# A two-layer attention trunk: x inside the first weight chunks, norms on VectorE by column halves, paired score products, attention steps in slots

## The chip, the cores and the metric

The kernel runs on one core of a Trainium2 chip. The metric is the device time of one execution in microseconds (us), as the median of runs; three runs of the kernel before gave 465.69, 466.3 and 468.05. Inside the core five engines work beside each other and wait for one another by semaphores: TensorE (PE, matmuls and transposes), VectorE (DVE), ScalarE (ACT), GpSimd (POOL) and SyncE (SP, which only issues DMAs here).

## The reference

A batch of one, 256 tokens of width 1024, and two layers in float32. The first layer runs retention (4 heads) and latent attention (8 heads whose scores have a 128-wide and a rotary 64-wide part) from one input projection; the second runs 16 heads of 64 columns, all of them causal over one block of 256 keys, so that no gathered block weighs anything. Both end in an output projection and a layer norm:

```python
def retention_mla_layer(x, pos, w_in, q_norm_g, w_uq, kv_norm_g, w_ukv, w_out):
    h = x @ w_in
    rq, rk, rv, rg, mq, mkv, mkr, mg = _split(h, EVEN_SPLITS)
    ...
    return jnp.concatenate([ret_out, mla_out], axis=-1) @ w_out

def moba_layer(x, pos, w_in, w_out):
    q, k, v, g = _split(x @ w_in, ODD_SPLITS)
    ...
    return (_merge(o) * jax.nn.silu(g)) @ w_out

for i in range(DEPTH):     # 2
    y = retention_mla_layer(...) if i % 2 == 0 else moba_layer(...)
    x = layer_norm(DN_ALPHA * x + y, ln_g[i], ln_b[i])
```

## The kernel before

**Arithmetic.** A float32 product is made of three passes: every operand is split into a high part (ACT copies it to a rounded type, L156) and a low part (DVE subtracts, L157), and `mm3` (L149 to L153) multiplies high by high (L151), low by high (L152 or L153, by which operand is which) and high by low. Weights are split in the same way as they arrive.

**Weights.** They are packed in the order of use into chunks of 512 KB (288 KB for the first eight). `load` (L169) fetches the next one on SP's queue into one of 4 raw buffers and splits it into one of 6 weight buffers, or into named spare ones.

**Start.** x comes transposed (`xt`) in four pieces of 256 KB on ACT's queue; eight chunks of 576 columns (queries' and keys' latents, tile names pm) are multiplied with it, 12 matmuls each. Constants, positions, norm gains and the decay table follow on ACT's queue, after the eight x splits in program order.

**Attention.** The small steps (scores, softmax, transposed probabilities, values) of retention, latent attention and the second layer are generators in one list `todo`; after each weight chunk of a projection `tick()` advances the first of them by one step, and `drain()` runs it empty. A scheduler of the framework then orders the instructions of each engine. The scores of a head (`causal_scores`, tile sc) are 3 passes for the first 128 queries against 128 keys and 3 for the second against 256; in latent attention each is followed by 3 passes of the rotary part, which has 64 contraction rows (kpe, qpe; two heads lie in the two halves of the 128 rows). In the second layer all score products have 64 rows (ck, cq).

**Output projections.** `out_proj` keeps the last TAIL = 4 chunks, does them for token tile 0 (128 tokens) first, then calls `between(0)`, which has tile 0's layer norm, and does them for tile 1 by pieces of columns. `layer_norm` divides its work by SPREAD: value 2 (tile 0 in either layer) squares on ACT and lets ACT and POOL do the second affine step, 1 (tile 1 of the first layer) squares on ACT alone, 0 (tile 1 of the second) is on DVE except for one power on POOL. In the first layer the normalised tile is transposed (pt, L708) and split into xT for the second layer, whose first five chunks (HOLD) are multiplied with tile 0 before tile 1 is needed. In the last call, tile 1's columns are done in pieces of 512, 256 and 256, each tile is normalised and stored in two halves on SP's and ACT's queues.

Of the kernel before, what the change touches and what calls it, by code (L numbers as in the profile page):

```python
# [32 lines left out]
TAIL = 4  # L33
HOLD = 5
WARM = 9
SPREAD = (2, 1, 2, 0)
# [9 lines left out]
def _plan():  # L46
    """The weight stream: per chunk its name, matrix, k tiles and columns."""
# [7 lines left out]
    block("m", "in0", _r(O_MQ, 256) + _r(O_MKR, 32) + _r(O_MKV, 256) + _r(O_MKR + 32, 32))  # L55
# [47 lines left out]
def _consts():  # L103
    """Constants of the shapes: identity, causal mask, decay tables, rotary frequencies."""
# [21 lines left out]
    return np.ascontiguousarray(np.concatenate(parts, 1))  # L126


CONSTS = _consts()
NCST = CONSTS.shape[1]  # L130
# [4 lines left out]
def trunk(ctx, tc, x, xt, pos, gq, gkv, lng, lnb, w, cst, dec, out):  # L135
# [13 lines left out]
    def mm3(o, a, b, ca, cb, start=False, stop=False):  # L149
        """o += a.T @ b by three passes of the split operands a, b (hi, lo)."""  # L150
        nc.tensor.matmul(o, ca(a[0]), cb(b[0]), start=start, stop=False, skip_group_check=True)  # L151
        nc.tensor.matmul(o, ca(a[1]), cb(b[0]), start=False, stop=False, skip_group_check=True)  # L152
        nc.tensor.matmul(o, ca(a[0]), cb(b[1]), start=False, stop=stop, skip_group_check=True)  # L153

    def split_to(hi, lo, src):
        nc.scalar.activation(hi, src, AF.Copy)  # L156
        nc.vector.tensor_tensor(lo, src, hi.bitcast(F32), op=OP.subtract)  # L157

# [8 lines left out]
    state = {"u": 0, "off": 0}  # L167

    def load(name, tags=None):  # L169
        tag, _, ks, cols = PLAN[state["u"]]  # L170
        assert tag == name, (tag, name)
        n = len(ks) * len(cols)
        raw = wp.tile([P, n], F32, name="raw", tag="raw", bufs=4)
        nc.sync.dma_start(raw, bass.AP(tensor=w.tensor, offset=w.offset + state["off"], ap=[[n, P], [1, n]]))
        state["u"] += 1
        state["off"] += n * P
        return ks, [t.rearrange("p (k c) -> p k c", c=len(cols)) for t in wsplit(raw, n, tags)]
# [8 lines left out]
    # work that waits for its turn between the chunks of the projections  # L186
    todo = []

    def tick(n=1):
        for _ in range(n):  # L190
            while todo:
                try:
                    next(todo[0])
                    break
                except StopIteration:
                    todo.pop(0)

    def drain():
        while todo:
            tick()  # L200
# [20 lines left out]
    pos_i = wk.tile([P, S], I32, name="pos_i", tag="neg", bufs=4)  # L221
    posn_i = cp.tile([P, NT], I32, name="posn_i")
    gqn = cp.tile([P, 2], F32, name="gqn")
    gkvn = cp.tile([P, 2], F32, name="gkvn")
# [8 lines left out]
    mask = cc("mask")  # L233

    # latent compression of queries and keys/values, shared rotary key
    pm = [[(pp, at)[j](f"pm{t}{j}") for j in range(2)] for t in range(NT)]
    xn = [cp.tile([P, DM], F32, name=f"xn{t}") for t in range(NT)]
    xr = [z.rearrange("p (k s) -> p k s", s=S) for z in xn]
    for k in range(0, KD, 2):
        nc.scalar.dma_start(xr[k // 4][:, k % 4:k % 4 + 2, :], xt[:, k:k + 2, :])  # L240
    for k in range(KD):
        split_to(xT_hi[:, k, :], xT_lo[:, k, :], xr[k // 4][:, k % 4, :])
        _, wv = load("m")
        for t in range(NT):
            for j in range(2):
                mm3(pm[t][j][:, :288], x_rows(k), wv, lambda z: z[:, t * P:(t + 1) * P],
                    lambda z: z[:, 0, j * 288:(j + 1) * 288], start=k == 0, stop=k == KD - 1)
    nc.scalar.dma_start(cs, cst)
    nc.scalar.dma_start(pos_i, bass.AP(tensor=pos.tensor, offset=pos.offset, ap=[[0, P], [1, S]]))
    for t in range(NT):  # L250
        nc.scalar.dma_start(posn_i[:, t:t + 1],
                            bass.AP(tensor=pos.tensor, offset=pos.offset + t * P, ap=[[1, P], [1, 1]]))
    nc.scalar.dma_start(gqn, gq)
    nc.scalar.dma_start(gkvn, gkv)
    nc.scalar.dma_start(decay, dec)

    def angles(dst_cos, dst_sin, ang, shape):
        """cos and sin of ang, brought to [-pi, pi] first."""
# [35 lines left out]
    def rope(src, t, nt, nh, dst, tag=None):  # L294
        """Half-split rotation of nh heads of 64 columns of nt token tiles from t on."""
# [13 lines left out]
    def transposed(srcs, n, hi, lo):  # L309
        """hi, lo (P, n, S) = the split transposes of the token tiles srcs[t] (P, n * P)."""  # L310
# [8 lines left out]
    lat = []  # L319

    def latents():
# [19 lines left out]
        yield  # L341
# [14 lines left out]
        yield  # L356
        pk = at("pk")
        for t in range(NT):
# [3 lines left out]
            nc.tensor.transpose(pk[:, t * P:(t + 1) * P], kd.rearrange("p a d -> p (a d)"), ident)  # L362
        lat.append(split(pk[:, :S], [P, S], "kpe"))
        yield
# [13 lines left out]
    def blockT_proj(name, o):  # L378
        """o (P, 2 * S) = the transpose of rows @ a block of 256 columns."""
# [9 lines left out]
    def gate(src, shape, name, bufs):  # L389
        """(tanh(g / 2) + 1) * g, twice silu(g)."""  # L390
# [5 lines left out]
    def rstd_of(stats, eps, half):  # L396
        """(var + eps) ** -0.5, halved where the gate is doubled, and -mean * that."""
# [11 lines left out]
    def retention(h, mid=None):  # L409
        """Projections of one retention head; its other steps go to todo as soon as they can."""  # L410
# [23 lines left out]
        def scores():  # L434
# [9 lines left out]
            yield  # L444

        def values():
            sT, v = got["sT"], got["v"]
# [12 lines left out]
            yield  # L460

        def merge():
            for t in range(NT):
                nc.vector.tensor_tensor(got["o"][t], got["o"][t], got["g"][t], op=OP.mult)
            hi = wk.tile([P, 4, S], F32R, name=f"rT{h}_h", tag="rT_h", bufs=2)
# [4 lines left out]
            yield  # L470

        todo.append(scores())
# [9 lines left out]
        todo.append(values())  # L482
# [3 lines left out]
        todo.append(merge())  # L486
# [26 lines left out]
    def causal_scores(o, prods):  # L513
        """o (P, 384) = scores of both query tiles; prods: (split queries, split keys, partitions)."""
        for t, a, n in ((0, 0, P), (1, P, S)):
            for i, (q, k, rs) in enumerate(prods):
                mm3(o[:, a:a + n], q, k, lambda y: y[rs, t * P:(t + 1) * P], lambda y: y[rs, :n],
                    start=t == 0 and i == 0, stop=i == len(prods) - 1)
# [8 lines left out]
    def av(o, pT, v, cols, start):  # L527
        """o (columns, S) = the transpose of probabilities @ values (of columns cols)."""
# [3 lines left out]
    def rotary_queries():  # L532
        """The rotary part of the queries of all latent-attention heads, transposed."""
# [14 lines left out]
        def later():  # L548
            transposed(qr, MH // 2, hi, lo)
            yield  # L550
        todo.append(later())
        tick()

    def mla(p):
        """Projections of a pair of latent-attention heads; the attention goes to todo."""
# [31 lines left out]
        def attend():  # L587
            sc = [at("sc") for a in range(2)]
# [261 lines left out]
```

## Time and profile before

| | |
|---|---|
| three runs | 465.69, 466.3 (median), 468.05 us |
| span of the profiled execution | 464.4 us; the page gives no other time of it |
| PE busy | 450.3 us, 97% |
| DVE, ACT, POOL busy | 73%, 51%, 3% |
| matmuls in the records | 2975 |
| HBM read | 74.01 MB |

The span runs from the first to the last instruction of the program; the time of a run also has what lies around it. A busy engine is one with an instruction in it: matmuls overlap, each lasts longer in the record than the distance to the next one, and so their pace is read from the distance of their starts.

### The profile page before, as it was taken

The numbers are of one execution on the slowest core, as the hardware profiler recorded it, in microseconds if no ns is written. First come the engines' busy times: TensorE is split into PE (matmuls) and PEld (weight loads), VectorE is DVE, ScalarE is ACT, GpSimd is POOL, SyncE is SP. The second block draws the span as 40 slices with busy tenths as digits, with TensorE's granted clock in tenths as the row PEclk, the third lists the DMA queues.
The fourth block names the chain that finished last, engine by engine and source line by source line (L and its number), as shares of the span: only waits on it lengthen the run. The fifth ranks groups of instructions, "written<-read, shape, count | busy, mean of one in ns | idle before, by whom it ended". The sixth has DMA issues, their size and how long they took to land.

```text
span 464.4 us, 7703 instructions
## 1 busy us (share of the span) xinstructions
PE 450.3 (97%) x2975; PEld 403.0 (87%) x2975; DVE 339.7 (73%) x658; ACT 236.0 (51%) x393; POOL 15.5 (3%) x22
## 2 busy tenths in 40 slices
PE   7999999999999999999999999999999999999993
PEld 4898899888999888889998888878999999999882
DVE  4889679785876866556596767655979798797836
ACT  5486464554644534345454646432646474644602
POOL 0010000000000000000000000020000000000003
PEclk9999999999989999999999999999999999999998
DMA  7987534544462556454445556824564435464002
GB/s 232 317 277 239 194 131 159 175 144 135 137 182 91 182 177 232 158 185 159 139 138 178 197 166 193 307 87 137 171 234 134 137 103 149 119 182 137 1 0 90
DMA packets 22787, 75.54 MB, mean 163 GB/s; under 512 B 3040, under 2 KB 3296, under 8 KB 22752
## 3 DMA queue, kind: packets, MB, share of 16 engines
q1 hardware_dynamic: 20016, 69.48, 46.6%
q10 hardware_dynamic: 2736, 5.59, 3.6%
q8 instruction: 23, 0.38, 0.3%
q14 instruction: 12, 0.10, 0.1%
HBM read 74.01 MB, written 1.05 MB: 162 GB/s over the span
## 4 chain that ended last, share of the span: by engine, by line
PE 94%; DMA 2%; DVE 2%; issue 0%; ACT 0%; DVEq 0%
PE pg L152 5%; PE pg L151 5%; PE pg L153 5%; PE pj L152 5%; PE pj L153 5%; PE pj L151 5%; PE acc L153 4%; PE acc L152 4%; PE acc L151 4%; PE pv L151 3%; PE pv L152 3%; PE pv L153 3%; PE pa L152 2%; PE pa L153 2%; PE pa L151 2%; PE sc L151 2%
## 5 line engine op out<-in xcount | busy, mean ns | idle before, releaser
L157 DVE TENSOR_TENSOR w_l<-raw,w_h 128x1024 fp32r<-128x1024 f32 (+2 forms) x134 | 157.6, 1180 | 64.0 <-ACT w_h L156 60.3
L156 ACT ACTIVATE w_h<-raw 128x1024 fp32r<-128x1024 f32 (+2 forms) x134 | 136.9, 1023 | 117.4 <-issue 38.0
L152 PE MATMUL pj<-w_h,xT_lo 128*128 128x256 f32 x192 | 54.3, 283 | 0.9 <-DVE xT_lo L157 0.9
L153 PE MATMUL pj<-w_l,xT_hi 128*128 128x256 f32 x192 | 54.3, 284 | 0.0
L151 PE MATMUL pj<-w_h,xT_hi 128*128 128x256 f32 x192 | 53.9, 284 | 0.0
L152 PEld LDWEIGHTS pj<-w_h,xT_lo 128*128 128x128 f32 x192 | 36.1, 188 | 1.1 <-DVE xT_lo L157 1.1
L153 PEld LDWEIGHTS pj<-w_l,xT_hi 128*128 128x128 f32 x192 | 36.1, 188 | 0.1
L151 PEld LDWEIGHTS pj<-w_h,xT_hi 128*128 128x128 f32 x192 | 35.8, 188 | 0.1
L151 PE MATMUL pv<-w_h,xT_hi 128*128 128x512 f32 x64 | 25.5, 399 | 0.0
L152 PE MATMUL pg<-w_h,xT_lo 128*128 128x512 f32 x64 | 25.4, 398 | 0.0
L152 PE MATMUL pv<-w_h,xT_lo 128*128 128x512 f32 x64 | 25.4, 397 | 0.0
L153 PE MATMUL pv<-w_l,xT_hi 128*128 128x512 f32 x64 | 25.4, 397 | 0.0
L153 PE MATMUL pg<-w_l,xT_hi 128*128 128x512 f32 x64 | 25.3, 399 | 0.0
L151 PE MATMUL pg<-w_h,xT_hi 128*128 128x512 f32 x64 | 25.3, 395 | 0.0
L500 DVE CUSTOM_DVE_ANT_0 neg<-sc,cs 128x128 f32<-128x128 f32 (+1 forms) x48 | 14.9, 355 | 9.4 <-PE sc L153 9.2
L503 ACT ACTIVATE prob<-neg,csm_m 128x128 f32<-128x128 f32 (+1 forms) x32 | 14.1, 443 | 11.0 <-DVE csm_m L500 11.0
L152 PE MATMUL pq<-xT_hi,w_l 128*128 128x256 f32 x64 | 18.5, 288 | 0.8 <-DVE w_l L157 0.8
L151 PE MATMUL pq<-xT_hi,w_h 128*128 128x256 f32 x64 | 18.8, 294 | 0.1
L152 PE MATMUL pkk<-xT_hi,w_l 128*128 128x256 f32 x64 | 18.6, 290 | 0.0
L151 PE MATMUL pkk<-xT_hi,w_h 128*128 128x256 f32 x64 | 18.6, 290 | 0.0
L153 PE MATMUL pkk<-xT_lo,w_h 128*128 128x256 f32 x64 | 18.5, 289 | 0.0
L152 PE MATMUL pg<-xT_hi,w_l 128*128 128x256 f32 x64 | 18.4, 287 | 0.0
(295 smaller groups left out, 1212.1 us busy)
## 6 DMA issues: line engine op xcount, KB each, us to landing
raw<-w SPq DMA_DIRECT2D x125, 512.0 KB, 3.6
raw<-w SPq DMA_DIRECT2D x8, 288.0 KB, 5.0
xn<-xt ACTq DMA_DIRECT2D x4, 256.0 KB, 7.1
raw<-w SPq DMA_DIRECT2D x4, 256.0 KB, 2.8
xn<-x ACTq DMA_DIRECT2D x2, 512.0 KB, 3.8
decay<-dec ACTq DMA_DIRECT2D x1, 512.0 KB, 5.0
decay_ln<-lng ACTq DMA_DIRECT2D x1, 512.0 KB, 4.2
rv_h_ln<-lnb ACTq DMA_DIRECT2D x1, 512.0 KB, 4.7
```

The source lines that it names most:

```text
L151: nc.tensor.matmul(o, ca(a[0]), cb(b[0]), start=start, stop=False, skip_group_check=True)
L152: nc.tensor.matmul(o, ca(a[1]), cb(b[0]), start=False, stop=False, skip_group_check=True)
L153: nc.tensor.matmul(o, ca(a[0]), cb(b[1]), start=False, stop=stop, skip_group_check=True)
L156: nc.scalar.activation(hi, src, AF.Copy)
L157: nc.vector.tensor_tensor(lo, src, hi.bitcast(F32), op=OP.subtract)
L500: nc.vector.tensor_tensor_reduce(out=neg[:, :b - a], in0=sc[j][:, a:b], in1=mask[:, S - b + a:], scale=-scale, scalar=3e38, op0=OP.add, op ...
L503: nc.scalar.activation(prob[:, j, a:b], neg[:, :b - a], AF.Exp, bias=nm[:, i, j:j + 1], scale=-1.0, accum_out=sm[:, i, j:j + 1])
```

## The change

- **x and constants.** x's eight 256-column pieces stand in front of the weights of the first chunks: 9 fetches, of 256 + 288, 288 and 7 times 832 columns, all issued at once on SP's queue into 4 raw buffers and 6 others. Positions and norm gains become columns of the constant table. Its DMA and the decay table's are issued on ACT's queue behind x's split number 2 and number 4.
- **Slots.** Every entry of `todo` has a tick at which it may go on; a generator yields how many ticks to wait (LAT1 to CAV) and 0 where an input is missing. Its step is issued after the last matmul so far.
- **Scores.** `causal_scores` has the 128-row products alone. `paired_scores` does the 64-row products of two heads, alternating between them.
- **Between the layers.** TAIL is 5. Tile 0's last chunks are multiplied by column halves too; the second layer's first five chunks are loaded before the norm of tile 0, and the last two chunks of tile 1's second half are issued after tile 0's transposes. `layer_norm` runs on DVE, each column half followed by its transposes; only tile 0 of the last norm squares on ACT.
- **End.** Tile 1's norm, affine steps and stores go by 512, 256 and 256 columns, and its first sum is issued after the affine step of tile 0 recorded in `state["normed"]`, which the call with t = 0 removes.

```diff
-TAIL = 4
+TAIL = 5
+LAT1, LAT2, QR, SCO, VAL, MRG, MSC, MPT, MAV, CROT, CSC, CPT, CAV = 3, 4, 2, 1, 1, 1, 1, 1, 1, 1, 1, 1, 1
-SPREAD = (2, 1, 2, 0)
...
+    def add(task, wait=1):
+        todo.append([state["tick"] + wait, task])
+    def tick():
+        state["tick"] += 1
+        for entry in list(todo):
+            if entry[0] > state["tick"]:
+                continue
+            try:
+                with tc.issue_after(state["mm"].ins):
+                    wait = next(entry[1])
+            except StopIteration:
+                todo.remove(entry)
+                continue
+            entry[0] = state["tick"] + (wait or 1)
+            if wait:
+                return
...
+    homes = [None] * 4 + [n + e for n in ("rqk", "mqk", "rv") for e in ("_h", "_l")]
+    first = [fetch("m", 0 if i == 1 else S, homes[i]) for i in range(KD + 1)]
+    for i, (raw, n, ks, cols) in enumerate(first):
+        k = ks[0]
+        if i != 1:
+            at_act = split_to(xT_hi[:, k, :], xT_lo[:, k, :], raw[:, :S])
+            for at_k, dst, src in ((2, cs, cst), (4, decay, dec)):
+                if k == at_k:
+                    with tc.issue_after(at_act.ins):
+                        nc.scalar.dma_start(dst, src)
...
+    def paired_scores(o, q, k, start):
+        for t, c, n in ((0, 0, P), (1, P, S)):
+            for i, (x, y) in enumerate(((0, 0), (1, 0), (0, 1))):
+                for a in range(2):
+                    rs = slice(a * MR, (a + 1) * MR)
+                    nc.tensor.matmul(o[a][:, c:c + n], q[x][rs, t * P:(t + 1) * P], k[y][rs, :n],
+                                     start=start and t == 0 and i == 0, stop=i == 2, skip_group_check=True)
...
         held = [load(name, spare[i] if i < len(spare) else None)[1] for i in range(last)]
-        for n in range(last):
-            part(n0 + n, held[n], 0)
+        ahead = [(n, load(n)) for n in nxt]
+        for cols in pieces[0]:
+            for n in range(last):
+                part(n0 + n, held[n], 0, cols)
         between(0, acc[0])
...
+            if "normed" in state:
+                with tc.issue_after(state.pop("normed").ins):
+                    return total(j, sl, **kw)
...
+        for j, sl in enumerate(parts):
+            if j > 1:
+                nc.vector.scalar_tensor_tensor(y[:, sl], y[:, sl], mv[:, 0:1], g[:, sl], op0=OP.subtract, op1=OP.mult)
+            state["normed"] = nc.vector.scalar_tensor_tensor(y[:, sl], y[:, sl], r[:, 0:1], b[:, sl],
+                                                             op0=OP.mult, op1=OP.add)
+            after(j, sl)
```

PE in the first layer, the scores of one pair of latent-attention heads: mqk is the 128-row part, 128x128 and 128x256 are the shapes of the outputs, kpe and qpe are the rotary 64-row part, `_h` and `_l` the high and low parts, and the number behind sc tells the head. Before:

```order
L153 MATMUL sc_2687<-mqk_l_2607,mqk_h_2606 128x128
L151 MATMUL sc_2687<-kpe_h_465,qpe_h_760 128x128
L152 MATMUL sc_2687<-kpe_h_465,qpe_l_761 128x128
L153 MATMUL sc_2687<-kpe_l_466,qpe_h_760 128x128
L151 MATMUL sc_2687<-mqk_h_2606 128x256
L152 MATMUL sc_2687<-mqk_h_2606,mqk_l_2607 128x256
L153 MATMUL sc_2687<-mqk_l_2607,mqk_h_2606 128x256
L151 MATMUL sc_2687<-kpe_h_465,qpe_h_760 128x256
```

Now, at the same place:

```order
L157 MATMUL sc_2681<-mqk_h_2599 128x256
L158 MATMUL sc_2681<-mqk_h_2599,mqk_l_2600 128x256
L159 MATMUL sc_2681<-mqk_l_2600,mqk_h_2599 128x256
L549 MATMUL sc_2680<-kpe_h_600,qpe_h_753 128x128
L549 MATMUL sc_2681<-kpe_h_600,qpe_h_753 128x128
L549 MATMUL sc_2680<-kpe_h_600,qpe_l_754 128x128
L549 MATMUL sc_2681<-kpe_h_600,qpe_l_754 128x128
```

The twelve 64-row products of a pair stood in four groups of three between 128-row products, and stand now in one group behind them, with the two heads in turn.

PE in the second layer, the first score products of two pairs of heads (ck and cq are keys and queries of 64 rows). Before:

```order
L151 MATMUL sc_3531<-ck_h_3420,cq_h_3412 128x128
L152 MATMUL sc_3531<-ck_h_3420,cq_l_3413 128x128
L151 MATMUL sc_3532<-ck_h_3420,cq_h_3412 128x128
L152 MATMUL sc_3532<-ck_h_3420,cq_l_3413 128x128
L151 MATMUL sc_3567<-ck_h_3420,cq_h_3412 128x128
```

Now:

```order
L549 MATMUL sc_3518<-ck_h_3407,cq_h_3399 128x128
L549 MATMUL sc_3519<-ck_h_3407,cq_h_3399 128x128
L549 MATMUL sc_3518<-ck_h_3407,cq_l_3400 128x128
L549 MATMUL sc_3519<-ck_h_3407,cq_l_3400 128x128
L549 MATMUL sc_3554<-ck_h_3407,cq_h_3399 128x128
```

The first pass of the second head moved ahead of the first head's second pass; what surrounds them is the same.

DVE at the end of the program: xn0 and xn1 are the two token tiles, acc the sums of the output projection, lmv and lr mean and scale of a norm, and lng, lnb its affine rows. Before:

```order
L658 SCALAR_TENSOR_TENSOR xn1_98<-xn1_98,acc_4915 128x512 [waits PE_49]
L654 TENSOR_SCALAR lr_5077<-lsm_5079 128x1 [waits Activation_49]
L666 SCALAR_TENSOR_TENSOR xn0_97<-xn0_97,lmv_5078,lng_ln1_3249 128x512 [waits DVE_49]
L666 SCALAR_TENSOR_TENSOR xn0_97<-xn0_97,lmv_5078,lng_ln1_3249 128x512
L660 BN_STATS lst_5135<-xn1_98 128x6 [waits DVE_49]
L658 SCALAR_TENSOR_TENSOR xn1_98<-xn1_98,acc_4916 128x512 [waits PE_49]
L660 BN_STATS lst_5135<-xn1_98 128x6 [waits DVE_49]
L661 BN_AGGR lmv_5134<-lst_5135 128x2 [waits DVE_49]
```

Now:

```order
L714 SCALAR_TENSOR_TENSOR xn0_93<-xn0_93,lmv_5059,lng_ln1_3266 128x512
L718 SCALAR_TENSOR_TENSOR xn0_93<-xn0_93,lr_5058,lnb_ln1_3268 128x512 [waits DVE_49,Pool_49]
L692 SCALAR_TENSOR_TENSOR xn1_94<-xn1_94,acc_4903 128x256 [waits PE_49]
L692 SCALAR_TENSOR_TENSOR xn1_94<-xn1_94,acc_4903 128x256
L718 SCALAR_TENSOR_TENSOR xn0_93<-xn0_93,lr_5058,lnb_ln1_3268 128x512 [waits DVE_49]
L692 SCALAR_TENSOR_TENSOR xn1_94<-xn1_94,acc_4902 128x512
L709 BN_STATS lst_5123<-xn1_94 128x6 [waits DVE_49] x3
L710 BN_AGGR lmv_5122<-lst_5123 128x2 [waits DVE_49]
```

Tile 1's three sums moved behind tile 0's subtract steps and first affine half, and the sum of its first 512 columns moved behind those of the last two 256-column pieces. The first of the sums waits for PE's last matmul.

## Rows read from the trace of the kernel before

**Rows 1.** The head of the page and two of its parts: span, and busy time, share and instructions of each engine.

```profile
span 464.4 us, 7703 instructions
...
PE 450.3 (97%) x2975; PEld 403.0 (87%) x2975; DVE 339.7 (73%) x658; ACT 236.0 (51%) x393; POOL 15.5 (3%) x22
```

**Rows 2.** The waits of PE: what waited, for what, and the sum, number and longest in us.

```profile
PE pm L151 <- ACT w_h L156: 2.3, 2, 2.1
...
PE pt L708 <- POOL xn L670: 0.9, 2, 0.6
PE pj L152 <- DVE xT_lo L157: 0.9, 1, 0.9
PE pq L152 <- DVE w_l L157: 0.8, 1, 0.8
```

**Rows 3.** The timeline of the start: start and duration in us, engine, line, operation, output and inputs, shape, and in brackets the idle time before and what ended it.

```profile
0.73 0.41 ACTq L240 DMA_DIRECT2D xn<-xt  x1
...
6.31 0.42 ACT L156 ACTIVATE xT_hi<-xn 128x256 fp32r<-128x256 f32 x1 [3.65 <-DMA xn<-xt]
6.64 0.67 ACT L156 ACTIVATE w_h<-raw 128x576 fp32r<-128x576 f32 x1
...
7.36 0.40 PE L151 MATMUL pm<-w_h,xT_hi 128*128 128x288 f32 x1 [2.09 <-ACT w_h L156]
...
13.53 0.68 ACT L156 ACTIVATE w_h<-raw 128x576 fp32r<-128x576 f32 x1 [1.81 <-DMA raw<-w]
...
20.96 1.23 DVE L157 TENSOR_TENSOR w_l<-raw,w_h 128x1024 fp32r<-128x1024 f32 x1 [0.63 <-PE pm L153]
...
22.24 0.39 PE L152 MATMUL pq<-xT_hi,w_l 128*128 128x256 f32 x1 [0.76 <-DVE w_l L157]
```

**Rows 4.** The DMA view of the first 12 us: GB/s moved in 40 slices of 0.3 us.

```profile
GB/s 0 0 0 0 0 31 84 77 211 224 253 262 167 172 179 207 327 310 399 383 394 387 445 396 404 415 409 399 403 370 406 353 243 72 51 89 119 202 200 140
```

**Rows 5.** The timeline of PE inside the scores of one latent-attention head (columns as in rows 3; 64*128 has 64 contraction rows).

```profile
252.81 0.27 PE L153 MATMUL sc<-mqk_l,mqk_h 128*128 128x128 f32 x1
253.01 0.33 PE L151 MATMUL sc<-kpe_h,qpe_h 64*128 64x128 f32 x1
253.18 0.27 PE L152 MATMUL sc<-kpe_h,qpe_l 64*128 64x128 f32 x1
253.29 0.27 PE L153 MATMUL sc<-kpe_l,qpe_h 64*128 64x128 f32 x1
253.49 0.38 PE L151 MATMUL sc<-mqk_h 128*128 128x256 f32 x1
253.71 0.28 PE L152 MATMUL sc<-mqk_h,mqk_l 128*128 128x256 f32 x1
```

**Rows 6.** A table of stretches. Columns: from and to, length, busy us (and instructions) of PE, PEld, DVE, ACT and POOL, granted clock, DMA share, GB/s. The second stretch is a block of latent-attention scores, the third what follows it, the fourth another such block, the fifth lies between the layers.

```profile
7.30:21.00 13.70, 13.36 (x97) 12.89 (x97) 11.80 (x35) 7.98 (x17) 0.00 (x0) 1.00 0.93 308
131.90:135.50 3.60, 3.60 (x24) 2.92 (x22) 2.09 (x6) 1.81 (x4) 0.00 (x0) 1.00 0.61 199
135.50:138.90 3.40, 3.40 (x15) 3.18 (x16) 1.77 (x10) 1.22 (x6) 0.00 (x0) 0.50 0.50 158
252.60:256.70 4.10, 4.10 (x27) 3.28 (x26) 2.75 (x8) 1.51 (x5) 0.00 (x0) 1.00 0.39 124
311.70:315.60 3.90, 2.14 (x14) 1.30 (x12) 3.43 (x8) 2.92 (x4) 1.89 (x2) 1.00 0.00 0
```

**Rows 7.** The timeline of PE in the second layer's scores; x2 is two instructions in one row.

```profile
343.72 0.33 PE L151 MATMUL sc<-ck_h,cq_h 64*128 64x128 f32 x2
343.89 0.28 PE L152 MATMUL sc<-ck_h,cq_l 64*128 64x128 f32 x2
```

**Rows 8.** The timeline between the layers: the first transposes of tile 0, and the first low pass behind tile 1's transposes.

```profile
312.42 0.66 PE L708 MATMUL pt<-cs,xn 128*128 128x128 f32 x4 [0.32 <-POOL xn L670]
...
315.53 0.38 PE L152 MATMUL pj<-w_h,xT_lo 128*128 128x256 f32 x1 [0.87 <-DVE xT_lo L157]
```

**Rows 9.** The timeline of the end. The last of PE's matmuls ends ahead of the row at 456.53.

```profile
451.59 0.69 DVE L647 SCALAR_TENSOR_TENSOR xn<-xn,acc 128x512 f32<-128x512 f32 x1
...
453.26 0.40 PE L153 MATMUL acc<-w_l,oT_h 128*128 128x512 f32 x1
...
453.49 0.28 PE L151 MATMUL acc<-w_h,oT_h 128*128 128x256 f32 x1
...
453.61 0.28 PE L152 MATMUL acc<-w_h,oT_l 128*128 128x256 f32 x1
...
454.36 1.41 DVE L666 SCALAR_TENSOR_TENSOR xn<-xn,lmv,lng_ln 128x512 f32<-128x512 f32 x2
454.67 0.82 POOL L663 TENSOR_TENSOR lr<-lr,mhalf 128x1 f32<-128x1 f32 x1 [137.28 <-DVE lr L654]
...
456.53 0.69 DVE L658 SCALAR_TENSOR_TENSOR xn<-xn,acc 128x512 f32<-128x512 f32 x1 [0.16 <-PE acc L153]
457.25 0.69 DVE L660 BATCH_NORM_STATS2 lst<-xn 128x6 f32<-128x512 f32 x1
...
458.29 1.75 DVE L666 SCALAR_TENSOR_TENSOR xn<-xn,lmv,lng_ln 128x512 f32<-128x512 f32 x2
...
459.96 1.41 DVE L672 SCALAR_TENSOR_TENSOR xn<-xn,lr,lnb_ln 128x512 f32<-128x512 f32 x2
```

**Rows 10.** The instructions of one line at the start that combine two tiles as the sums of the norm do: number, then shortest, median and longest duration in ns.

```profile
L270 DVE SCALAR_TENSOR_TENSOR ang<-ang_k,ang x5: 421/426/427, 17.8 to 22.3; 128x256 f32<-128x256 f32 x5
```

More of the change, by code (lines that the diff above doesn't have):

```diff
@@ L187, in trunk, with until @@
     todo = []
[L189 to L199, printed above, removed]
+    def add(task, wait=1):
[14 more added lines that the diff above has]
+                return
+    def until(ready):
+        while not ready():
             tick()
@@ L469, in merge @@
                 catT[4 * h + i] = (hi[:, i, :], lo[:, i, :])
-            yield
-        todo.append(scores())
+            yield 1
+        add(scores(), SCO)
         if mid:
@@ L548, in later @@
         def later():
+            while 3 not in catT:
+                yield 0
             transposed(qr, MH // 2, hi, lo)
-            yield
-        todo.append(later())
+            got_qpe.append(1)
+            yield 1
+        add(later(), QR)
         tick()
@@ L604, in attend, with out_proj @@
                 catT[16 + 2 * p + i] = (hi[:, i, :], lo[:, i, :])
-            yield
-        todo.append(attend())
-    def out_proj(name, ks, src, last, between, pieces, spare=()):
+            yield 1
+        add(attend(), MSC)
+    def out_proj(name, ks, src, last, between, pieces, spare=(), nxt=""):
         acc = [[pp("acc") for j in range(2)] for t in range(NT)]
@@ L620, in out_proj @@
             _, wv = load(name)
-            if ks[n] not in src:
-                drain()
+            until(lambda: ks[n] in src)
             for t in range(NT):
@@ L680, in affine_rows @@
         return pair
-    todo.append(latents())
+    add(latents())
     for h in range(RH):
@@ L700, in trunk, with turn @@
     rows = affine_rows(0, ("decay", "rv_h"))
+    halves = [slice(j * 512, (j + 1) * 512) for j in range(2)]
     def after_even(t, acc):
-        layer_norm(xn[t], acc, 1.0, *rows, SPREAD[t])
-        for d in range(0, KD, 4):
+        def turn(j, cols):
+            d = 4 * j
             pt = at("pt")
@@ L745, in third @@
             oT[2 * q + d] = split(og, [P, S], f"oT{2 * q + d}")
-        for f in (first, second, third):
+        while "kT" not in got:
+            yield 0
+        for f, wait in ((first, CPT), (second, CAV), (third, 1)):
+            if f is third:
+                while "g" not in got:
+                    yield 0
             for d in range(2):
                 f(d)
-            yield
+            yield wait
     def odd_chunk(name, o, wv, ks, tiles):
@@ L799, in trunk, with store, _pack @@
         got["g"] = gate(pg, [P, 512], "cgate", 2)
+    quarters = [slice(0, 512), slice(512, 768), slice(768, 1024)]
     def after_odd(t, acc):
[L802 to L807 removed]
+        def store(j, cols):
+            (nc.sync, nc.scalar, nc.sync)[j].dma_start(out[t * P:(t + 1) * P, cols], xn[t][:, cols])
+        if t == 0:
+            state.pop("normed")
+        layer_norm(xn[t], acc, ALPHA, *rows, t == 0, quarters if t else halves, store)
+    out_proj("o1", _r(0, 8), oT, TAIL, after_odd,
+             ((((0, 512),), ((512, 1024),)), (((0, 512),), ((512, 768),), ((768, 1024),))))
     assert state["u"] == len(PLAN)
[L811 removed]
+def _pack(mats, xt):
     out = []
[L814 removed]
+    for u, (name, m, ks, cols) in enumerate(PLAN):
         a = mats[m].reshape(-1, P, mats[m].shape[1])
[L816 removed]
+        a = a[ks][:, :, cols].transpose(1, 0, 2).reshape(P, -1)
+        if name == "m" and u != 1:
+            a = np.concatenate([xt[ks[0]], a], 1)
+        out.append(a.reshape(-1))
     return np.concatenate(out)
```

195 lines of the change are left out of this document (97 added, 98 removed).

## The prediction

> **What bounds the kernel now.** I read the page's engine line first: TensorE (PE) is busy 450.3 of 464.4 us, VectorE (DVE) 73%, ScalarE (ACT) 51% [rows 1]. So time goes away only where PE stops, where PE's own instructions come slower than they could, or before its first and after its last matmul. The list of PE's waits, read next, is short: about 4.9 us in four entries, at the start (pm, pq) and between the layers (pt, pj) [rows 2]. The timeline of those places gives their causes [rows 3, 8], the timeline of the score products shows PE slow while it counts as busy [rows 5], and a table of stretches shows the one place at half clock [rows 6]. Last I read what follows the last matmul [rows 9].
>
> The sum is made against the profiled execution, whose page gives a span of 464.4 us and no time beside it; the median of the runs is 466.3 (465.69 to 468.05). I take the 1.9 between them as what lies around the span and leave it alone. The measurement cannot tell less than about 0.5%, 2.3 us, from no change.
>
> **The start.** x's first piece is issued at 0.73 and is there at 6.31, together with the first weight chunk; split and first matmul follow at 7.36 [rows 3]. What lands first is 256 KB of x and 288 KB of weights side by side. The rate row (0.3 us a slice) reaches those 544 KB at about 4.8 us and half of them at about 3.4 [rows 4]. A first transfer of 272 KB alone in front should thus land up to 1.4 us earlier; the bounds are 6.3 (nothing gained, the slowest of the transfer's parts decides) and 4.9, and I take 5.2, near the row. Behind it ACT has x (0.33 until the next can start) and 288 columns (0.4) where it had 576 (0.67) [rows 3]: first matmul 0.8 after landing, not 1.05. Then 96 matmuls: before, 97 took 13.36 us busy and the stretch 13.7 [rows 6], with a 0.3 to 0.5 stop at 13.53 for a chunk that was issued late because it waited for a buffer [rows 3]. Now all nine chunks are queued at once into buffers of their own. A chunk has 416 KB, which at 390 GB/s (the plateau of rows 4) is 1.1 us against 1.6 us on PE (12 matmuls of 0.133), and the table (340 KB) and decay (512 KB), now issued on ACT's queue behind x of chunks 2 and 4, add 2.2 us to the last chunk, which still lands about 10.5 us after the first where PE wants it at 12.2. The next layer's chunks stand behind all nine on SP's queue; the first of them is there at about 12, split by ACT and DVE (1.06 and 1.23) at about 14.1, 0.2 late. Pass two of pq thus starts at 5.2 + 0.8 + 13 + 0.4 = 19.4 against 22.24: **2.8 saved** (1.7 to 3.1 by the landing).
>
> **Latent-attention scores.** Four head pairs, 24 products each. Inside one kind a product follows the last by 0.11 to 0.12 us [rows 5, 9]; from 128 contraction rows to 64 the step is 0.20 and the next 0.17, and back it is 0.20 and 0.22 [rows 5]. A round trip costs 0.35 us. The order of before makes four round trips in a pair of heads, that of the change one (two in the first pair): three fewer, 1.05 us, and 0.7 in the first. The twelve 64-row products now alternate between the two halves of the rows. That two such products run side by side is seen in the second layer, two starts merged in one row [rows 7]; so twelve steps become six: 0.68 us. Together 3 x 1.73 + 1.38, **6.6 in all** (3.9 if they do not run side by side).
>
> The half clock from 135.5 to 138.9 follows directly on such a block; the granted clock is 0.50 there, 1.2 of 2.4 GHz, and 15 matmuls fill 3.40 us [rows 6], of which half, at most 1.7, is the clock's: I take 1.5 us. The block at 252.6 ran at the full clock [rows 6], so it is not certain that the block is the cause; it is the only thing near it, and the block shrinks from 4.1 to 2.4 us. I count **1.5 saved**, bounds 0 and 1.5, and another fall as a rival.
>
> **Second-layer scores: nothing.** The name says paired products, but in the order of before the second head's first product stands behind the first head's second one, and yet the trace starts the two first passes together and the two second passes 0.17 later [rows 7]. PE already ran the two row halves beside each other; with either order 24 products fill about 14 steps. I put 0, bounds 0 and -5.4 (below).
>
> The Trainium skill, TensorE: Matmul & The Clock Gate, Part 3 (The mechanism), says that matmuls start and end in program order, "strict FIFO, no reordering". The trace does not agree: two products that are not neighbours in the order start within one row [rows 7]. By that rule the old order could not have paired and the change would save the pairing here too; that is the fourth rival.
>
> **Between the layers.** In 311.70 to 315.60 PE is busy 2.14 of 3.90 us [rows 6]: it waits for POOL's and ACT's share of tile 0's norm and then for a split that stood behind a weight split on DVE [rows 2, 8]. Now the norm is on DVE alone, its first half's statistics lie under the second column half's 15 matmuls, and PE has 24 matmuls of 0.23, 5.6 us [rows 9], between tile 0's last product and the transposes. From the rows at the end of the kernel, sum, statistics, aggregate, power and first affine half take 456.53 to about 460.7, 4.2 us, the second half 0.7 more [rows 9]: covered with 0.7 to spare. The ACT share vanishes; the five weight chunks are split earlier, in buffers that the order frees in time. Tile 1's norm, 4.9 us, lies under 58 products of 0.12, 6.8 us; after its transposes PE waits about 0.3 for the low split. 1.76 to 2.2 gone less 0.3: **1.8 saved** (if the first cover fails by a microsecond, 0.8).
>
> **The end: it costs.** In the order of DVE the first sum of tile 1's last columns now stands behind tile 0's first affine half, and behind it come tile 0's other half and tile 1's 512-column sum, which before was done ahead of PE's end. From tile 0's second sum (451.59) the power ends 3.9 and the two subtract steps 4.2 later [rows 9], so tile 1's sums can start at 4.8; PE ends 3.7 after that sum (3 steps of 0.23 and 27 of 0.12, less the 0.25 by which the sum follows its matmul). DVE is 1.1 late. Then two 256-column sums (0.36 each, between the 0.42 of such an operation on 256 columns [rows 10] and half of the 0.69 of 512), 0.66, 0.61, statistics 0.36 + 0.36 + 0.73, aggregate 0.34, 1.67 to the first affine piece as before, pieces 0.66 + 0.38 + 0.43: 6.9 us against 456.53 to 461.37, 4.8 [rows 9]. **3.2 lost**, bounds 0 (if the wait is not as the order reads) and 4. The smaller last store saves at most 0.1.
>
> At no cost I put the constants' merging, the paired operands and the steps in slots: between a head pair's scores and its first probability transpose stand at least 38 matmuls (35 before), 4.4 us. If the softmax outlasts that, each of twelve blocks loses 0.3.
>
> **Sum.** -2.8 - 6.6 - 1.5 - 0 - 1.8 + 3.2 = -9.5: span 454.9, time 456.8.
>
> **Rivals.**
> 1. The 64-row halves do not run side by side in the first layer and the clock falls again somewhere: +2.7 + 1.5, 461.0. For: the columns are other tiles; against: rows 7. 12%.
> 2. The slots starve PE: softmax late in twelve blocks (3.6) and transposes between the layers waiting 1 us: 461.4. For: DVE's 73%, now with the norms; against: the order's distances. 7%.
> 3. The end is not longer, because tile 0's norm ends before PE does: 453.6. For: only the order speaks against it; DVE's steps there are timed by rows of the same operations, so 8%.
> 4. The second layer pairs only now: 6 steps of 0.11 in each of eight pairs of heads, 5.4 us: 451.4. 5%.
> 5. Slower: more 64-row products side by side let the clock fall behind each of the twelve blocks, 1.5 us each, eighteen in all: 474.8. It passes 466.3 from seven falls on. For: the one fall stands behind such a block. Against: the other blocks ran at full clock and all get shorter or stay. 4%.
> 6. The gains are eaten by waits I do not see, 464 to 468: 4%.
>
> The forecast itself has 60%, with a range of its own of 454.5 to 459.5. Out of these cases faster by over 0.5% is 0.60 + 0.12 + 0.07 + 0.08 + 0.05 = 0.92, within 0.5% 0.04, slower 0.04. The range 453 to 461.5 leaves out rivals 4 to 6 and some edges.
>
> **What would show it.** First pm matmul near 6.0 us and pq's second pass near 19.4; a block of latent scores in 2.4 us with row pairs merged; no half clock at 135; second-layer blocks as long as now; PE idle under 0.6 us between the layers; the last matmul about 11.4 us before the end of the span, not 8.2, with DVE still on tile 0 when it ends. A first matmul after 7, latent blocks over 3 us, or new entries of over 1 us in PE's waits would prove the forecast wrong.

## The result

The changed kernel takes 453.76 us (median of 4; 453.49 to 454.44) against 466.84 beside it: a ratio of 0.9724, interval 0.9694 to 0.9754. The forecast was 456.8. The profiled execution has a span of 451.7, 12.7 less.

The head of the page and the only two waits that PE has left, to compare with [rows 1, 2]:

```profile
span 451.7 us, 7694 instructions
...
PE 439.5 (97%) x2978; PEld 396.2 (88%) x2978; DVE 341.6 (76%) x663; ACT 231.4 (51%) x386; POOL 12.8 (3%) x18
```

```profile
PE pidle L234 <- DVE idle L231: 1.2, 1, 1.2
PE pm L157 <- ACT w_h L162: 0.5, 1, 0.5
```

PE works on the same products in 11 us less of busy time (450.3 to 439.5): most of the gain is where PE counted as busy before.

**Start** (timeline; [rows 3]). The first split begins at 3.58 where it began at 6.31, and the first product at 4.71, not 7.36:

```profile
3.58 0.42 ACT L162 ACTIVATE xT_hi<-raw 128x256 fp32r<-128x256 f32 x1 [1.35 <-DMA raw<-w]
...
4.71 0.72 PE L157 MATMUL pm<-w_h,xT_hi 128*128 128x288 f32 x2
...
7.23 0.40 PE L157 MATMUL pm<-w_h,xT_hi 128*128 128x288 f32 x1 [0.47 <-ACT w_h L162]
...
18.60 0.28 PE L158 MATMUL pq<-xT_hi,w_l 128*128 128x256 f32 x1
```

The chunk that PE needs next is late by 0.47, and pq's second pass, which waited before, follows at once: 18.60 against 22.24.

**Latent scores** (timeline of PE; [rows 5]). One change to 64 rows, then pairs of products in the two row halves; x2 is both heads:

```profile
214.67 0.28 PE L159 MATMUL sc<-mqk_l,mqk_h 128*128 128x256 f32 x1
214.88 0.33 PE L549 MATMUL sc<-kpe_h,qpe_h 64*128 64x128 f32 x2
215.04 0.28 PE L549 MATMUL sc<-kpe_h,qpe_l 64*128 64x128 f32 x2
...
215.76 0.39 PE L158 MATMUL pq<-xT_hi,w_l 128*128 128x256 f32 x1
```

**Stretches** (columns as in [rows 6]): the block at the place of the one at 131.90, what follows it, now at the full 2.4 GHz, and the transposes between the layers, where PE is busy for all of the 2.55 us.

```profile
127.90:130.25 2.35, 2.35 (x26) 2.09 (x24) 1.01 (x1) 1.06 (x1) 0.00 (x0) 1.00 0.59 213
130.25:133.65 3.40, 3.40 (x30) 3.40 (x29) 2.29 (x14) 2.90 (x9) 0.00 (x0) 1.00 0.57 167
...
298.90:301.45 2.55, 2.55 (x16) 2.16 (x16) 1.69 (x3) 1.09 (x2) 0.00 (x0) 1.00 0.00 0
```

Tile 0's first affine half there, and its transposes (timeline; [rows 8]):

```profile
297.54 0.74 DVE L718 SCALAR_TENSOR_TENSOR xn<-xn,lr,rv_h_ln 128x512 f32<-128x512 f32 x1
...
299.19 1.03 PE L758 MATMUL pt<-cs,xn 128*128 128x128 f32 x8
```

**End** (timeline of PE's last product, before and now, and of DVE now; [rows 9]):

```profile
456.22 0.27 PE L153 MATMUL acc<-w_l,oT_h 128*128 128x256 f32 x1
```

```profile
441.13 0.28 PE L159 MATMUL acc<-w_l,oT_h 128*128 128x256 f32 x1
```

```profile
437.69 0.68 DVE L692 SCALAR_TENSOR_TENSOR xn<-xn,acc 128x512 f32<-128x512 f32 x1
...
441.53 0.74 DVE L718 SCALAR_TENSOR_TENSOR xn<-xn,lr,lnb_ln 128x512 f32<-128x512 f32 x1
442.19 0.74 DVE L692 SCALAR_TENSOR_TENSOR xn<-xn,acc 128x256 f32<-128x256 f32 x2
442.85 0.74 DVE L718 SCALAR_TENSOR_TENSOR xn<-xn,lr,lnb_ln 128x512 f32<-128x512 f32 x1
443.51 0.68 DVE L692 SCALAR_TENSOR_TENSOR xn<-xn,acc 128x512 f32<-128x512 f32 x1
444.11 1.34 DVE L709 BATCH_NORM_STATS2 lst<-xn 128x6 f32<-128x256 f32 x3
...
447.28 1.53 DVE L718 SCALAR_TENSOR_TENSOR xn<-xn,lr,lnb_ln 128x512 f32<-128x512 f32 x3
```

When PE ends, DVE is still on tile 0; tile 1's sums start 1.06 after PE's last product starts, where 0.31 was enough before (456.53 behind 456.22). From that product to the span's end it is 10.6, not 8.2. The row at 437.69 is tile 0's second sum: PE's last product starts 3.44 behind it, where it was 4.63 before (456.22 behind 451.59).

### The profile page after: what moved, and what is told of

The parts are those of the page before. It is cut to its first block, busy times and chain, and to the rows that moved or that the text cites. A ratio compares the mean times of both kernels' runs of the same rounds, so it can differ in the third digit from the quotient of the medians.

```text
span 451.7 us, 7694 instructions
## 1 busy us (share of the span) xinstructions
PE 439.5 (97%) x2978; PEld 396.2 (88%) x2978; DVE 341.6 (76%) x663; ACT 231.4 (51%) x386; POOL 12.8 (3%) x18
## 4 chain that ended last, share of the span: by engine, by line
PE 95%; DVE 2%; DMA 1%; ACT 1%; issue 0%; SPq 0%; DVEq 0%
PE pg L157 5%; PE pg L158 5%; PE pg L159 5%; PE pj L158 5%; PE pj L157 5%; PE pj L159 5%; PE acc L157 4%; PE acc L158 4%; PE acc L159 4%; PE pv L157 3%; PE pv L159 3%; PE pv L158 3%; PE sc L549 3%; PE pa L158 2%; PE pa L159 2%; PE pa L157 2%
## 5 line engine op out<-in xcount | busy, mean ns | idle before, releaser
L163 DVE TENSOR_TENSOR w_l<-raw,w_h 128x1024 fp32r<-128x1024 f32 (+3 forms) x134 | 156.1, 1169 | 57.8 <-ACT w_h L162 56.4
L162 ACT ACTIVATE w_h<-raw 128x1024 fp32r<-128x1024 f32 (+3 forms) x134 | 135.6, 1016 | 93.9 <-issue 20.2
L157 PE MATMUL pg<-xT_hi,w_h 128*128 128x256 f32 x64 | 18.2, 285 | 0.0
```

Source lines behind the costliest of these rows:

```text
L162: done = nc.scalar.activation(hi, src, AF.Copy)
```

## The experiments

All start from the changed kernel unless said. Sums over a block of scores add the distance from each product's start to the next start. Among the eleven profiles that have the changed kernel's start, or a variant of it, pq's first product stands anywhere from 18.5 to 19.6; so what an edit is worth below a microsecond is read from stretches of the profile and not from the times. The stretch from pq's first product to PE's last repeats well: it is 422.64 to 422.65 us long in five profiles, two of the changed kernel and three of versions that edit only the start or the end.

**The order inside the latent scores.**

```diff
             for a in range(2):
-                causal_scores(sc[a], [z[:, a, :] for z in qn], [z[:, a, :] for z in kn])
-            paired_scores(sc, [z[:, p, :] for z in qpe], kpe, False)
+                mixed_scores(sc[a], (([z[:, a, :] for z in qn], [z[:, a, :] for z in kn], slice(0, P)),
+                                     ([z[:, p, :] for z in qpe], kpe, slice(a * MR, (a + 1) * MR))))
```

> Only the latent scores go back to the old order: per head three 128-row and three 64-row products in turn, the heads one after the other; all else is the changed kernel (453.8 us; its four latent blocks take 9.48 us where they took 15.65). Theory: the blocks cost by changes between 64 and 128 rows and by products of 64 rows that do not run beside each other; they come back to about 15.2 us, +5.7: 459.5 us, and 461 if a stretch at half clock comes back behind one of them. Rival: the explicit slots, not the order inside the block, made the difference; then the blocks stay under 11 us and the time under 455.5.

`mixed_scores` has the order of before, three 128-row and three 64-row products in turn. 461.75 us. The four blocks take 15.74 again, and half clock (0.50, 1.2 GHz) is back. It begins inside the last products of the second block (128.90 to 133.20) and lasts 3.4 us. The kernel before has the same: its block ends at 136.24, so that the stretch at half clock in [rows 6] begins inside it, not behind it.

```profile
132.50:135.90 3.40, 3.40 (x15) 3.18 (x16) 1.81 (x10) 1.18 (x6) 0.00 (x0) 0.50 0.46 157
```

The theory stands, and the block's order is shown to bring the clock down. Not every run need pay the same for it: the mean granted clock of seventeen runs of the kernel before goes from 0.984 to 0.995.

**Grouped, but head by head** (`for a in range(2)` moved outermost in the 64-row products).

> The 64-row products of a latent pair stay in one group behind the 128-row ones, but head by head instead of alternating. Theory of the prediction: PE starts a product of one row half beside one of the other half also where they are a few places apart, but six places apart is too far, so the pairing (24 steps of 0.107, 2.6 us) is lost and the grouping (about 3.6 us) stays: 456.3 us. Rival: the pairing does not depend on the order; then the blocks stay at 9.5 us and the time at 453.8.

455.24 us; blocks 10.48, between the two theories. PE pairs the middle products. At 216.77 the second head's first product (`kpe_h,qpe_h`) starts beside the first head's third (`kpe_l,qpe_h`), which stands four places ahead of it in the program's text; the other start in that row of two is the first head's fourth. The order that the scheduler gave PE in this run is not on record.

```profile
216.49 0.32 PE L558 MATMUL sc<-kpe_h,qpe_h 64*128 64x128 f32 x1
216.66 0.27 PE L558 MATMUL sc<-kpe_h,qpe_l 64*128 64x128 f32 x1
216.77 0.27 PE L558 MATMUL sc<-kpe_l,qpe_h 64*128 64x128 f32 x1
216.77 0.43 PE L558 MATMUL sc<-kpe_h,qpe_h 64*128 64x128 f32 x2
```

So 1.0 of the 6.2 us comes from the alternating order; the other 5.2 from grouping, from what PE pairs by itself and from the clock, which no run parts.

**The second layer's scores, head by head.**

> Only the second layer's scores go back to head by head, as before. Theory: PE pairs most of them anyway, as it did before (8.34 us for 96 products against 7.90 now): +0.4 us, 454.2. Rival: the pairing there is new and the rest of the second layer's gain (1.5 us from its second quarter on) hangs on it: +1.5, 455.3. The fourth rival of the prediction would want +5.4, 459.2.

453.92 us; its blocks take 8.34, to the hundredth what they took before, against 7.90. The alternating order is worth 0.44 there, and the quick steps of the rest of the layer do not hang on it (115.3 ns a step of 256 columns, 115.4 with it). That the time is near the theory's 454.2 is luck: pq's first product is 0.6 later than in the changed kernel's profile, and the end is 1.2 shorter, 9.4 us from PE's last product. The edit has no line there. But PE's work is in another order at the end: its last product stands 4.63 behind tile 0's second sum, as before the change, not 3.44, and tile 1's sums start 0.54 behind it.

```profile
437.56 0.69 DVE L701 SCALAR_TENSOR_TENSOR xn<-xn,acc 128x512 f32<-128x512 f32 x1 [0.47 <-PE acc L159]
...
442.19 0.28 PE L159 MATMUL acc<-w_l,oT_h 128*128 128x256 f32 x1
...
442.73 1.35 DVE L701 SCALAR_TENSOR_TENSOR xn<-xn,acc 128x512 f32<-128x512 f32 x3
```

**No slots** (the step in `tick` is no longer issued behind the last matmul).

> The attention steps keep their slots in the program but are no longer issued behind the last matmul before them: the scheduler places them freely, as before the change. Theory: the steps' places cost nothing and gain nothing, 453.3 to 454.3 us. Rival: the explicit places are what took the last 1 to 1.5 us out of the second layer (softmax steps that meet weight splits on DVE): 455 us or more, with new waits of PE for probabilities.

454.52 us, no new wait of PE. The time is within the noise of the theory's upper edge, but in the profile pq's first product to PE's last takes 423.25, 0.6 more than the 422.65. That lies in the pace of the second layer's products of 256 columns, 116.2 ns a step against 115.4. This stretch holds 62 products, and 65 in the changed kernel (shown under the weight buffers below):

```profile
312.40:319.50 7.10, 7.10 (x62) 7.10 (x62) 6.39 (x10) 5.01 (x5) 0.00 (x0) 1.00 0.69 224
```

So the slots are worth about 0.6 in this profile, by the order of the work and not by a wait; why the order changes the pace stays open.

**The end without the edge** (`state.pop("normed")` for both tiles; the edge is what puts tile 1's first sum behind tile 0's affine step).

> The changed kernel without the edge at the end that puts tile 1's first sum behind tile 0's affine step; the scheduler now puts tile 1's 512-column sum and its statistics, and the first 256-column sum, ahead of PE's end, and tile 0's affine halves between tile 1's statistics. Theory: in the changed kernel DVE aggregates tile 1 4.4 us after PE's last matmul starts (445.48 against 441.13) because the sums stand behind tile 0; here about 3.0: 1.4 less, 452.4 us. Rival: DVE has the same work either way and the end only changes its order: 453.8.

454.74 us: the rival. DVE meets tile 1's first 256-column sum early (in the program's order its own fifteen products are done by 440.7) and waits 1.62, until PE's last product is done; tile 0's steps stand behind the wait. In the kernel both 256-column pieces lie in one tile of PSUM, the memory that PE writes, which would explain it; no run gave them tiles of their own.

```profile
442.50 0.42 DVE L692 SCALAR_TENSOR_TENSOR xn<-xn,acc 128x256 f32<-128x256 f32 x1 [1.62 <-PE acc L159]
442.84 0.15 DVE L704 TENSOR_SCALAR lr<-lsm 128x1 f32<-128x1 f32 x1
442.90 1.41 DVE L714 SCALAR_TENSOR_TENSOR xn<-xn,lmv,lng_ln 128x512 f32<-128x512 f32 x2
```

From PE's last product (442.19) to the end it is 10.7, as with the edge. The edge fills a wait that would be there without it.

**Tile 0's second affine step on ACT and POOL as well.**

> As without the edge, and tile 0's second affine step goes to ACT (scale) and POOL (add), as it was before the change. Theory: tile 1's aggregate then comes about 1.6 us after PE's last matmul starts instead of 4.4; but its power on POOL stands behind tile 0's two additions there (1.27 each) and comes 2.2 us earlier than now, not 2.8: 451.6 us. Rival: POOL frees no time on DVE because tile 1 waits for POOL longer than it gains: 453 or more.

454.88 us, the end 10.9: the same wait, and then tile 1's power behind POOL's two additions, which take 2.93 together here, where I had counted on 1.27 each from the kernel before:

```profile
444.72 2.93 POOL L720 TENSOR_TENSOR xn<-xn,lnb_ln 128x512 f32<-128x512 f32 x2 [0.83 <-ACT xn L719]
447.62 0.72 POOL L712 TENSOR_TENSOR lr<-lr,mhalf 128x1 f32<-128x1 f32 x1
```

**Four chunks held, tile 0 not by halves** (`TAIL = 4`).

> Between the layers four chunks are held instead of five and tile 0 takes its last chunks over both column halves at once, as before the change; the norm stays on VectorE with its transposes by halves. Theory of the prediction: the cover of tile 0's norm shrinks by six matmuls of 0.23 (1.4 us) and its first half's statistics (1.4 us) come behind the last matmul; 0.9 to spare now, so PE waits about 1.9 us for the transposes: 455.7. Rival: the norm on one engine is what matters, the cover is ample: 453.8 with no wait of PE there.

455.69 us. PE waits 0.2 at tile 0's transposes and 0.2 at the second layer's first products, not 1.9; from the first acc product to the second layer's first pg one it takes 0.8 longer (54.25 against 53.44). The end is longer by 0.4 as well, since `TAIL` is used there too, and the start is later by 0.6: that the time meets the theory's 455.7 is luck.

```profile
300.11 0.44 PE L758 MATMUL pt<-cs,xn 128*128 128x128 f32 x2 [0.22 <-DVE xn L718]
```

The cover matters as the theory says, at less than half its price, and half of the 0.8 stands in the two waits.

**Where the weight buffers lie** (a 32-byte tile in front of them, and of all that is placed behind it).

> Only 32 bytes a partition are put in front of the weight buffers, so that they start at a multiple of 64 bytes again, as before the change (which moved them to 32 beyond one). The second layer's 256-column projections run there at steps of 0.113 to 0.114 us in some stretches of the changed kernel, 0.117 in all of the kernel before. Theory: the place of the buffers does that: 0.117 in all stretches, about +0.9, 454.7 us. Rival: the order of the work around them does it: the same fast stretches, 453.8.

455.65 us. The same stretch of projections holds 65 products in the changed kernel and 63 here:

```profile
312.40:319.50 7.10, 7.10 (x65) 7.10 (x65) 6.47 (x9) 4.67 (x5) 0.00 (x0) 1.00 0.78 235
```

```profile
312.40:319.50 7.10, 7.10 (x63) 7.10 (x62) 6.55 (x9) 4.11 (x5) 0.00 (x0) 1.00 0.73 228
```

From pq's first product to PE's last it takes 424.3 us instead of 422.6: 1.6 for 32 bytes, more than the theory's 0.9. The second layer's mean step of 256 columns goes from 115.4 to 118.0 ns, the first layer's the other way, from 117.9 to 117.4.

**The same 32 bytes in the kernel before.**

> The kernel before with 32 bytes a partition put in front of its weight buffers, so that they start 32 bytes beyond a multiple of 64, as in the changed kernel. Theory: the place of these buffers lets the second layer's 256-column projections run at 0.113 us a step in some stretches instead of 0.117, so that about 1.3 us of the change's gain has nothing to do with what was edited: 1.0 to 1.7 less than the kernel before. Rival: the fast pace needs the changed order as well; no such stretch, the same time.

464.05 us against 466.81 beside it, ratio 0.9935 (0.9909 to 0.9961). The place alone makes that kernel faster too, by more than the theory's 1.0 to 1.7 and not where the theory had it: its mean step of 256 columns falls from 118.4 to 116.3 ns in the first layer and hardly in the second (117.2 to 116.9), where the change's own gain lies (117.2 to 115.4). So the rival holds in part: the second layer's pace needs more of the change than the place. In its profile half clock begins inside another latent block, the fourth, and lasts twice as long:

```profile
251.76:258.58 6.82, 6.82 (x18) 5.29 (x19) 3.34 (x12) 2.42 (x8) 0.00 (x0) 0.50 0.33 132
```

**The old start.**

> The changed kernel with the start of before: x in four pieces on ACT's queue, eight whole chunks of 576 columns on SP's, the merged table and the decay table behind them. Theory: two queues at once share the rate, the first pair is whole at about 6.1 us instead of 3.5, first matmul at about 7.3 instead of 4.7, and the first low split of the next weights is late again by 0.9: pq's second pass at 22.2, 2.6 to 3.6 later than now, 456.4 to 457.4 us. Rival: the 27 fewer small transfers of the constants made the first pair quicker, not the queue; then the first matmul is at 5 to 6.

457.06 us; pq's second pass at 22.29, the first product at 7.76:

```profile
7.76 0.40 PE L157 MATMUL pm<-w_h,xT_hi 128*128 128x288 f32 x1 [2.51 <-ACT w_h L162]
...
8.52:11.94 3.42, 3.42 (x17) 3.42 (x16) 3.29 (x8) 2.96 (x9) 0.00 (x0) 0.50 1.00 356
```

x's first piece landed at 6.69, the weights beside it at 5.82, against 3.56 for the one transfer of the new start. The small transfers are gone here as well, so they do not make the first pair late. Nor do its 544 KB alone: the new start has 832 KB landed by 6.16. What is left is that the first pair comes on two queues, with later pieces of both in between. That agrees with the Trainium skill, DMA: Bandwidth & Descriptors, Queues, rings and completion order: a DMA engine takes packets of its queues in turn. The second row shows that half clock can follow an idle PE as well (2.51 us without work, then 0.76 of products at full clock); it spoils the sum a little (pq's second pass itself no longer waited).

**The changed kernel again, and a version with two edits.**

> The changed kernel itself once more, beside the next three on one chip. From pq's first matmul to PE's last one it took 422.6 us; the start (pq's first matmul at 18.5) was up to 1.1 later in eight variants with the same start, by when the second and third chunk landed. 453.5 to 454.6 us.

454.14 us (453.53 to 455.21), pq's first product at 19.1.

```diff
-        for cols in mcols if k == 0 else (mcols[0] + mcols[1],):
+        for cols in mcols if k < 2 else (mcols[0] + mcols[1],):
...
+        state["tile0"] = state["mm"]
         between(0, acc[0])
+        tile0 = state["tile0"]
...
+                    if name == "o1" and n >= last - 3:
+                        order.enter_context(tc.issue_after(tile0.ins))
...
-        if t == 0:
-            state.pop("normed")
+        state.pop("normed", None)
...
+            if square and j == 0:
+                nc.scalar.activation(y[:, sl], y[:, sl], AF.Copy, scale=r[:, 0:1])
+                nc.gpsimd.tensor_tensor(y[:, sl], y[:, sl], b[:, sl], op=OP.add)
```

> The changed kernel with two edits. The second k tile of x and weights is also split (x with 288 columns, then 288), so that PE finds it sooner: 0.5 us less at the start. At the end, tile 1's products with the last three chunks stand behind tile 0's last product, the edge from tile 0's affine step to tile 1's sums is dropped, and one half of tile 0's second affine step goes to ACT and POOL. Theory: the end costs because DVE's work for tile 0 reaches past PE's last matmul; with 4.9 us of PE's work behind tile 0's last product instead of 3.7, and 0.7 us of DVE's given away, tile 1's 256-column sums start when PE ends, and the end of the span comes 8.9 us after PE's last matmul starts, not 10.6: 451.6 us with the start. Rival: DVE's work after PE's end is set by tile 1's own chain, and the end stays over 10 us: 453.3.

452.1 us (451.94 to 452.68), ratio to before 0.9678 (0.965 to 0.9706): faster than both kernels. The end takes 8.3 from PE's last product (441.79):

```profile
441.87 0.73 DVE L726 SCALAR_TENSOR_TENSOR xn<-xn,lr,lnb_ln 128x512 f32<-128x512 f32 x1
442.52 0.74 DVE L696 SCALAR_TENSOR_TENSOR xn<-xn,acc 128x256 f32<-128x256 f32 x2
443.18 0.74 DVE L713 BATCH_NORM_STATS2 lst<-xn 128x6 f32<-128x256 f32 x2
...
445.75 1.53 DVE L726 SCALAR_TENSOR_TENSOR xn<-xn,lr,lnb_ln 128x512 f32<-128x512 f32 x3
```

From the 256-column sums to the last affine step's end it is 4.8 instead of 6.6: tile 0's half (0.66), tile 1's 512-column sum (0.60) and its statistics (0.61) are out of that chain. The three edits to the end were not tried apart. The start gained nothing: the second tile came sooner, the next one is late instead.

```profile
8.87 0.40 PE L157 MATMUL pm<-w_h,xT_hi 128*128 128x288 f32 x1 [0.75 <-ACT w_h L162]
```

## Why the prediction was right, and where not

| term | forecast | measured | from |
|---|---|---|---|
| start | -2.8 | -3.6 | pq's second pass, 22.24 to 18.60 |
| latent scores | -6.6 | -6.2 | four blocks, 15.65 to 9.48; 0.3 of it is half clock inside the second |
| half clock | -1.5 | -1.2 | twelve products behind that block, 2.72 to 1.52; with the 0.3 above -1.5 |
| second-layer scores | 0 | -0.4 | four blocks, 8.34 to 7.90 |
| between the layers | -1.8 | -2.3 | first acc to the next pg product, 55.70 to 53.44 |
| end | +3.2 | +2.4 | PE's last product to the end, 8.2 to 10.6 |
| rest | 0 | -1.4 | what is left of -12.7 |

The signs are those forecast; the 3.2 between -9.5 and -12.7 comes from sizes and from a term put at nothing, and most of them lie in one direction. So the time, 453.76, is inside 453 to 461.5, by 0.8, and below the 454.5 to 459.5 that I gave the forecast itself. It stands beside the 453.6 of the third rival, whose end without loss did not come: that it lies there is chance.

**The start** was mis-sized by the landing: I took 5.2, with 4.9 as the earliest, from the bytes that the rate row of two mixed queues showed [rows 4]; alone in front, 272 KB landed at 3.56. Half of that 1.6 was lost again: the first product came 1.15 after the landing, not 0.8, behind the last of the warm-up matmuls on an idle tile (4.64), and the next chunk was late by 0.47. How late varies: pq's first product stood at 18.5 to 19.6 in the eleven profiles with that start or its variant with the second tile split. The 18.48 of this profile is the earliest of them; at their median the start would be worth 3.0, next to the 2.8 forecast, from a landing that was far off and waits that I had not counted. The low split of pq, put 0.4 late, was on time.

**The latent scores** are right in size and cause: the old order gives 15.74 again. The part that I gave to running side by side (2.7) is not all due to alternating, which is worth 1.0, since PE finds pairs itself over some places; what grouping alone is worth (3.9 forecast) no run shows. **The half clock**, of whose cause I was not certain, comes from the block's order: it came back with the old order, in the kernel before with 32 bytes more it began in another such block, and none of the eleven profiles with the 64-row products grouped has it in one or behind one. So rivals 1 and 5 fall: more products side by side do not bring the clock down.

**The second layer**: nothing was the right side of the bounds; the fourth rival (5.4) falls with 0.44. The rule in program order of the Trainium skill (TensorE: Matmul & The Clock Gate, Part 3, The mechanism) again does not agree, as far as the program's text is the order: head by head, PE starts a second head's product ahead of the first head's later ones (216.77).

**Between the layers** the cover held with 0.9 to spare: tile 0's affine step ends at 298.28, its transposes stand at 299.19. Some of the 2.3 is the quicker step of the last row of the table.

**The end**: the order was read rightly, DVE is late and the old chain is longer, so the third rival falls. The lateness is 0.75, not 1.1, the chain 6.62, not 6.9, and the last store gives 0.13. What I did not see is that the edge is not the cause: without it DVE waits instead. About half of the 2.4 comes from how little of PE's work stands behind tile 0's last product: where it was 4.63 instead of 3.44, with the edge in place (the second layer's scores head by head), the end was 9.4. The other half is that tile 1's 512-column sum and its statistics come behind PE's end there too. With both changed, and a half of tile 0's second step off DVE, it is 8.3 in the version with two edits.

**The rest** is what no row of before could tell: the change moved the weight buffers from a multiple of 64 bytes to 32 beyond one, and the second layer's steps got shorter. 32 bytes more, which bring the buffers back to such a multiple, cost 1.6. I had put the merged constants at nothing, which moved them. But the place is not the whole cause: the same shift in the kernel before left the second layer's steps nearly as they were, and without the slots a stretch of quick steps was gone at the same place. The slots starved nothing, so the second rival falls.

## What to carry to other kernels

Order products so that changes of row count are few and neighbours use different row halves; the gain is in PE's pace, where no list of waits shows it. Put what the first product needs alone in front of one queue. At the end, count the last engine's work from the last product of the tile before, and look whether a piece that is to be read early shares its PSUM tile with a later one (a tile of its own was not tried here). Before crediting an edit with a third of a per cent, shift the buffers by 32 bytes and look again.

## What the runs showed that I had not expected

- 32 bytes of buffer address are worth 0.4 to 0.65%, a loss in one kernel and a gain in the other: steps of 256 columns of 115.4 ns in the second layer against 118.0. Most stretches of quick steps (0.113 to 0.114) lie at the same products in the variants that keep the place, but not all: without the slots the first of them is gone. Why some and not others stays open.
- PE pairs 64-row products of the two halves that stand up to four places apart in the program's text.
- Half clock of 3.4 us, or twice that, begins late in a block with four round trips between 128 and 64 rows a head pair, not always the same block; what in the block causes it was not tried apart.
